# Hybrid attention and convolution block: some depthwise taps summed by adding transfers, attention cut into steps, plain pointwise products

## The chip, the core and the metric

One core of a Trainium2 chip runs the whole block once. The metric is device time in microseconds (us), from launch to end, as the median of several runs. Shapes are written partitions x elements. TensorE (PE) does matrix products, VectorE (DVE) and ScalarE (ACT) do elementwise work, GpSimd (POOL) does very little here, and SyncE (SP) issues the loads. PEld in the profile is TensorE's weight load, which runs beside its matmuls.

## What is computed

One layer over 256 tokens of width 4096, all in float32. Attention has 16 heads of 128; the convolution module has 2048 channels and 31 causal taps.

```python
xn   = rms_norm(h, norm_in_g)
proj = xn @ w_in                                  # 4096 -> 7 x 2048: q k v z_a a_c g_c z_c
y_a  = chunked_attention(q, k, v, rel_table)      # chunks of 64, all earlier chunks in the band
y_a  = rms_norm(y_a, attn_out_g) * silu(z_a)
u    = a_c * sigmoid(g_c)
u    = sum over k of w_dw[k] * u shifted by 30-k tokens, + b_dw      # depthwise, 31 taps
u    = silu(layer_norm(u))
y_c  = rms_norm(u @ w_pw + b_pw, conv_out_g) * silu(z_c)
h    = h + concat(y_a, y_c) @ w_out
h    = h + sigmoid(rms_norm(h) @ w_ple_gate + b) * (p @ w_ple)
out  = rms_norm(h, final_g)
```

## The kernel before

**Products.** Each float32 operand is split into a high part, which fits TensorE's fast float32 format, and the low rest; a product is three matmuls (high x high, low x high, high x low). `mixed_product` makes two column blocks of 512 at a time for all 256 tokens, over 16 *units* of 256 rows of the weight (8 units for the pointwise product). For a unit it loads two 512 KB tiles `wt` (128x1024), ACT casts each to `wh` (`parts_of`, L204) and DVE subtracts to get `wl` (L205). A plain unit has 24 matmuls of 512 columns. A unit marked `*` (a "seven") uses a Strassen-like scheme with 7 sub-products in place of 8, so 21 matmuls, and in exchange DVE makes sums of weights (`ua`, `ub`, L427 to L432) that are cast and subtracted too (`uh`, `ul`), and combinations of the left operand (`comb`). Buffers: five `wt`, three each of `wh` and `wl`, two each of `uh` and `ul`.

**Order of the work.** First come ten groups of `w_in` columns: `glu_conv(0)` and `(1)` (the convolution's input), `keys(0)`, `values(0)`, `attention(0)`, `glu_conv(2)` and `(3)`, `keys(1)`, `attention(1)`, `keys(2)`, then q and v (`attention(2)` after it), then k and v (`attention(3)` after it). Then the pointwise product with `w_pw` in two halves (`point`), four `gated` groups, four groups with `w_out` and four with `w_ple_gate`.

**Deferred work.** Small steps wait in the queue `later`; `fill(n)` pops n of them after each unit, n coming from a table such as `early_fills`. Each `glu_conv(c)` puts its 4 x 31 taps there (`conv_tap`, L681: one DVE instruction multiplies a shifted row block by a tap's weight and adds it to `cv`). `layer_norm_swish` puts the normalisation there: sums, `mean`, `center`, `square`, `variance`, `spread`, `swish` (ACT's Silu on 128x256, L785) and `split` (L795, L796), which makes the left operand `uS` of the pointwise product.

**Attention** handles 4 heads (`attention(g)`), head after head: scores on TensorE (L841, L842), scale, bias and maximum on DVE (L848, L852), Exp on ACT (L853), three transposes (L860), a copy by DVE (L862), the product with v (L865 to L867), a scaling by ACT (L869).

A scheduler fixes each engine's order when the program is built; it moves instructions past each other as dependences allow, except where `pin` keeps the program's order or `tc.issue_after(i)` puts the instructions of a block, on i's engine, behind i. At run time each engine runs its list strictly in order. Transfers issued by SP go in order too; each waits for its tile to be free. A tile is free when its last reader is done; `act` has eight buffers shared by `xin`, `cv`, `qT`, `y_c`.

Of the kernel before, what the change touches and what calls it, by code (L numbers as in the profile page):

```python
# [10 lines left out]
F32 = mybir.dt.float32  # L11
F32R = mybir.dt.float32r
AF = mybir.ActivationFunctionType
ALU = mybir.AluOpType
# [11 lines left out]
def hybrid_block(  # L26
# [152 lines left out]

    later = deque()  # L180

    def fill(n):
        for _ in range(min(n, len(later))):
            later.popleft()()

# [13 lines left out]
    def parts_of(wt, kc, tiles=None):  # L199
        if tiles is None:  # L200
            tiles = part_tiles()
        wh, wl = tiles
        made = (
            nc.scalar.copy(wh[:, :kc, :], wt[:, :kc, :]),  # L204
            nc.vector.tensor_tensor(  # L205
                wl[:, :kc, :], wt[:, :kc, :], wh[:, :kc, :].bitcast(F32), ALU.subtract
            ),
        )
        return (wh, wl), made

# [112 lines left out]

    early_fills = (4, 6, 7, 1, 5, 1, 5, 1, 5, 1, 2, 4, 6, 6, 6, 4)
    final = units("1 0* 3 2* 5 4* 6* 7 8* 9 10* 12* 11 13 14 15")
    late = units("1 3 5 7 9 11 13 15 0* 2 4* 6 8* 10* 12 14")

    def mixed_product(
# [67 lines left out]
        for n, (pair, seven) in enumerate(order):  # L396
# [9 lines left out]
            if n >= len(order) - n_left:  # L406
                for k in range(2):
                    tiles = left[2 * (n - len(order) + n_left) + k]
                    held.append((2 * pair + k, parts_of(wts[k], 2, tiles and tiles())[0]))
                fill(fills[n % len(fills)])  # L410
                continue
            if not seven:
                for k in range(2):
                    add_plain(n, k, *parts_of(wts[k], 2)[0])
                fill(fills[n % len(fills)])
                continue
# [39 lines left out]
            if n == last_seven:  # L456
                on_helpers(helper)
            fill(fills[n % len(fills)])
        after.close()
# [213 lines left out]
    conv = []  # L673

    def conv_tap(cv, uT, i, b, k):
        if k == PAD:
# [3 lines left out]
        else:  # L680
# [3 lines left out]
            )  # L684

    def glu_conv(c):
        if c == 0:
# [3 lines left out]
        else:  # L691
            sg, gate = scaled_pair(
                w_in0, o_a + c * NB, o_g - o_a, early, r_x, early_fills,
                
# [27 lines left out]
    def layer_norm_swish():  # L722
# [13 lines left out]
        def mean(s):  # L736

            m = tmp_psum()
            nc.tensor.matmul(m[:, :T], mean_w, fold(s), start=True, stop=True)
            stat("mu", m[:, :T])  # L740
# [20 lines left out]
        def variance(s):  # L761

            s = fold(s)
            m = tmp_psum()
# [6 lines left out]
            rsqrt(st["r"], m[:, :NH], 1)  # L771

        def spread(s):

            m = tmp_psum()
            for h in range(NH):
                d = s[:, 0, h * P : (h + 1) * P]
                nc.vector.tensor_scalar(d, ident, st["r"][:, h : h + 1], None, ALU.mult)
                nc.tensor.matmul(m[:, h * P : (h + 1) * P], mean_w, d, start=True, stop=True)
# [20 lines left out]
        later.extend(partial(total, c) for c in range(n))  # L800
        later.append(lambda: mean(st["s"]))
# [4 lines left out]
        later.append(lambda: variance(st["q"]))  # L806
        later.extend(rest)
        later.append(lambda: spread(st["s"]))
        later.extend(rest)
# [26 lines left out]
    def attention(g):  # L836
        qT, kT, v, bias = qs[g], ks.pop(g), vs.pop(g), biases.pop(g)
        y = qT.rearrange("q g (h d) -> q h g d", h=NH)
        for hd in range(GH):
# [4 lines left out]
            nm = spool.tile([P, NH], F32, tag="nm", name="nm")  # L844
            den = spool.tile([P, NH], F32, tag="den", name="den")
            for h, (lo, hi) in enumerate(((0, P), (P, P + T))):
# [8 lines left out]
                    accum_out=den[:, h : h + 1],  # L855
                )
            nc.vector.reciprocal(den, den)
            pt = tmp_psum()
            for j in range(3):
                nc.tensor.transpose(pt[:, j * P : (j + 1) * P], s[:, j * P : (j + 1) * P], ident)  # L860
            pT = spool.tile([P, 3 * P], F32, tag="pT", name="pT")
            nc.vector.tensor_copy(pT, pt[:, : 3 * P])  # L862
            o = tmp_psum()
            vc = slice(hd * HD, (hd + 1) * HD)
# [7 lines left out]
        for h in range(NH):  # L872
            square_sum(ssq_a[:, h, g : g + 1], y[:, h])
        y_a.append(y)
# [6 lines left out]
    def load_bias(g):  # L881
# [9 lines left out]
        )  # L891
        nc.gpsimd.memset(bias[: P // 2, :, : P // 2], NEG)

# [19 lines left out]
    def late_pool():  # L913
# [15 lines left out]
    load_bias(1)  # L929
    keys(1, early_fills)  # L930
    attention(1)
    keys(2, early_fills)
    layer_norm_swish()
    load_bias(2)
# [3 lines left out]
    k, vs[3] = blocks(  # L938
        (o_k + 3 * NB, o_v + 3 * NB), valued, (5, 5, 4, 5, 4, 2, 3, 2, 3, 2, 3, 4, 4, 4, 4, 4),
        then=late_pool,  # L940
    )
    keyed(3, k)
    attention(3)
    r_a = rstd_of(ssq_a, AW, "r_a")


# [10 lines left out]

    point = units("1 3 4 5 0* 6 2* 7"), units("0 1 2 3 4 5 6 7")
    uC = {}
    for c in range(2):  # L960
        uC[2 * c] = act.tile([P, 2, 2, T], F32R, tag="act", name="comb_u"), 0
        scratch = spool.tile([P, 2, NB], F32, tag="stage", name="comb")
        combine_again(*uC[2 * c], uS[c], 0, (scratch[:, 0], scratch[:, 1]))()
    first_scratch.close()
    spool = upool = pool("lpool", 2, side=1)
    y_c = []
    ssq_c = cpool.tile([P, NH, CW // NB], F32, name="ssq_c")
    for c0, order in zip(range(0, CW // NB, 2), point):
        row = broadcast_row(b_pw, c0 * NB, 2 * NB, tag="stage")
        rows = [row[:, j * NB : (j + 1) * NB] for j in range(2)]  # L970
        ys, z = [], []

        def y_tiles():
            ys.extend(act.tile([P, NH, NB], F32, tag="act", name="y_c") for _ in range(2))

        def on_helpers(helper):
            y_tiles()
            z.extend([ys[j][:, h, :] for j in range(2)] for h in range(NH))
            tt(z[0][0], helper["P1"], rows[0], ALU.add)
            helper_sums(helper, z)  # L980
            for h, j in QUARTERS[1:]:
                tt(z[h][j], z[h][j], rows[j], ALU.subtract if j else ALU.add)

        acc = mixed_product(w_pw[0], c0 * NB, uS, uC, order, on_helpers)
        if not z:
            y_tiles()
        for h, j in QUARTERS:
            y = ys[j][:, h, :]
            if z:
                tt(y, acc[h][j], y, ALU.subtract if j else ALU.add)  # L990
            else:
                tt(y, acc[h][j], rows[j], ALU.add)
            square_sum(ssq_c[:, h, c0 + j : c0 + j + 1], y)
        y_c.extend(ys)
    nc.scalar.activation(idle_out, ssq_c[:, 0, 1:2], AF.Silu)
    r_c = rstd_of(ssq_c, CW, "r_c")
# [304 lines left out]
```

## Time and profile before

| What | Value |
|---|---|
| Median of 3 runs | 2039.21 us (2038.81 to 2040.08) |
| The profiled execution | 2041.64 us, its span 2039.9 us |
| PE, PEld | 99%, 81% busy |
| DVE, ACT, POOL | 95%, 58%, 0% busy |
| Loads of weights and x | 406 MB read, 201 GB/s over the span; 16 transfer engines 63% busy |
| `w_in` groups after the first, about 80 to 880 us | DVE 773 us and ACT 428 us busy of 800 |
| Pointwise product, about 880 to 1000 us | DVE 103 us and ACT 74 us busy of 120 |

A row of a group gives line, engine, operation, tiles (out<-in), count, busy time and mean nanoseconds of one, then the engine's idle time before them and what ended it. A busy TensorE is not TensorE at its best: a 512-column matmul is recorded with some 390 ns but the next one starts long before it ends, so what counts is the distance between starts. `<-` in waits and timelines names what the waiting engine was released by.

### The profile page before, as it was taken

To read this page: it belongs to the slowest core of one execution; us is meant where nothing else is said; L and a number is where in the kernel's file an instruction comes from. 1 tells how busy PE (TensorE), PEld (TensorE's weight loads), DVE (VectorE), ACT (ScalarE), POOL (GpSimd) and SP (SyncE) were. 2 spreads that over 40 slices of the span, in tenths; PEclk is the share of its full clock that TensorE was granted. 3 is DMA by queue.
4 is the path that set the end of the run, shared out by engine and by line. 5 is a ranking of instruction groups with operands and counts; after the bars stand their busy time and mean duration, and the time that the engine had idled before them with its cause. 6 is when DMAs were issued, how large, how long until landed. Compare 5 with 4: busy or idle time off the path is not lost.

```text
span 2039.9 us, 26023 instructions
## 1 busy us (share of the span) xinstructions
PE 2018.6 (99%) x9088; PEld 1657.7 (81%) x9088; DVE 1929.4 (95%) x2760; ACT 1190.0 (58%) x1537; POOL 8.5 (0%) x19
## 2 busy tenths in 40 slices
PE   9999999999999999999999999999999999999997
PEld 7888888888888888877888888888888888888876
DVE  7999999989999999988899999999999999999998
ACT  7655545655555545576556556676565666655555
POOL 0000000000000000000000000000000000000000
PEclk9999999999999999999999999999999999999999
DMA  8666666566665666655666666676666656666765
GB/s 290 191 197 205 201 193 201 170 197 195 205 200 163 196 197 185 191 165 195 185 221 199 196 217 200 218 237 205 208 208 202 211 188 209 196 220 206 235 208 179
DMA packets 157758, 412.30 MB, mean 202 GB/s; under 512 B 12974, under 2 KB 16190, under 8 KB 157626
## 3 DMA queue, kind: packets, MB, share of 16 engines
q1 hardware_dynamic: 156976, 409.80, 63.2%
q8 instruction: 71, 1.16, 0.2%
q10 hardware_dynamic: 650, 0.84, 0.1%
q14 instruction: 61, 0.50, 0.1%
HBM read 406.39 MB, written 4.19 MB: 201 GB/s over the span
## 4 chain that ended last, share of the span: by engine, by line
PE 52%; DVE 2%; issue 1%; DMA 1%; ACT 0%; POOLq 0%; POOL 0%; ACTq 0%; DVEq 0%
PE acc L371 38%; PE acc_P L371 12%; PE acc L218 1%; DVE wl L205 1%; PE tmp_ps L170 1%; DMA wt<-in_w_in_dram 0%; DVE ul L205 0%; PE acc L359 0%; DMA wt<-in_w_out_dram 0%; ACT wh L204 0%; DVE ub L431 0%; DVE hc L1100 0%; DVE ua L428 0%; PE tmp_ps L860 0%; PE tmp_ps L842 0%
## 5 line engine op out<-in xcount | busy, mean ns | idle before, releaser
L371 PE MATMUL acc<-wh,big_t 128*128 128x512 f32 x4224 | 1308.3, 392 | 5.0 <-ACT wh L204 2.6
L204 ACT CAST wh<-wt 128x1024 fp32r<-128x1024 f32 (+1 forms) x737 | 711.8, 976 | 539.4 <-PE acc L371 401.5
L371 PEld LDWEIGHTS acc<-wh,big_t 128*128 128x128 f32 x4224 | 791.0, 188 | 169.8 <-ACT wh L204 4.5
L205 DVE TENSOR_TENSOR wl<-wt,wh 128x1024 fp32r<-128x1024 f32 (+1 forms) x737 | 819.9, 1124 | 36.2 <-ACT wh L204 32.3
L371 PE MATMUL acc<-wl,big_t 128*128 128x512 f32 x2112 | 814.7, 391 | 0.0
L371 PEld LDWEIGHTS acc<-wl,big_t 128*128 128x128 f32 x2112 | 396.5, 188 | 84.2 <-DVE wl L205 1.8
L204 ACT CAST uh<-ub 128x1024 fp32r<-128x1024 f32 x128 | 134.6, 1052 | 127.7 <-DVE ub L432 103.7
L681 DVE SCALAR_TENSOR_TENSOR cv<-uT,dw,cv 128x249 f32<-128x249 f32 (+22 forms) x480 | 207.6, 460 | 0.6
L204 ACT CAST uh<-ua 128x1024 fp32r<-128x1024 f32 x128 | 134.8, 1053 | 85.4 <-DVE ua L428 80.1
L205 DVE TENSOR_TENSOR ul<-ub,uh 128x1024 fp32r<-128x1024 f32 x128 | 156.0, 1219 | 8.4 <-ACT uh L204 7.8
L371 PE MATMUL acc_P<-uh,big_t 128*128 128x512 f32 x528 | 161.8, 392 | 0.0
L205 DVE TENSOR_TENSOR ul<-ua,uh 128x1024 fp32r<-128x1024 f32 x128 | 155.8, 1218 | 0.2 <-ACT uh L204 0.2
L371 PEld LDWEIGHTS acc_P<-uh,big_t 128*128 128x128 f32 x528 | 98.0, 188 | 23.0 <-ACT uh L204 3.4
L427 DVE TENSOR_TENSOR ua<-wt 128x512 f32<-128x512 f32 x128 | 87.7, 685 | 23.1 <-DMA wt<-in_w_in_dram 16.6
L371 PE MATMUL acc_P<-ul,big_t 128*128 128x512 f32 x264 | 101.6, 393 | 0.2
L428 DVE TENSOR_TENSOR ua<-wt 128x512 f32<-128x512 f32 x128 | 87.4, 683 | 5.7 <-DMA wt<-in_w_out_dram 3.1
L432 DVE TENSOR_TENSOR ub<-ub,wt 128x512 f32<-128x512 f32 x128 | 87.6, 684 | 0.8
L431 DVE TENSOR_TENSOR ub<-ua,wt 128x512 f32<-128x512 f32 x128 | 87.4, 683 | 0.3
L371 PE MATMUL acc<-uh,big_t 128*128 128x512 f32 x256 | 79.2, 390 | 0.0
L371 PE MATMUL acc_P<-wh,big_t 128*128 128x512 f32 x256 | 79.1, 389 | 0.0
L371 PE MATMUL acc_P<-uh,comb_t 128*128 128x512 f32 x228 | 70.2, 391 | 0.1
L371 PEld LDWEIGHTS acc_P<-ul,big_t 128*128 128x128 f32 x264 | 49.4, 188 | 13.6 <-DVE ul L205 3.3
(230 smaller groups left out, 1343.7 us busy)
## 6 DMA issues: line engine op xcount, KB each, us to landing
wt<-in_w_in_dram SPq DMA_DIRECT2D x447, 512.0 KB, 4.1
wt<-in_w_out_dram SPq DMA_DIRECT2D x128, 512.0 KB, 4.2
wt<-in_w_ple_gate_dram SPq DMA_DIRECT2D x128, 512.0 KB, 4.1
wt<-in_w_pw_dram SPq DMA_DIRECT2D x32, 512.0 KB, 4.8
hc<-in_x_dram SPq DMA_DIRECT2D x8, 512.0 KB, 6.0
wt<-in_w_ple_dram SPq DMA_DIRECT2D x8, 512.0 KB, 4.4
xin<-in_x_dram SPq DMA_DIRECT2D x7, 512.0 KB, 8.3
out_dram<-hc SPq DMA_DIRECT2D x12, 256.0 KB, 2.5
```

The costliest lines, as they stand in the source:

```text
L170: nc.tensor.transpose(pt[:, i * T + h * P : i * T + (h + 1) * P], src[:, h, b] if len(src.shape) == 4 else src[:, h, b * P : (b + 1) * P], ...
L204: nc.scalar.copy(wh[:, :kc, :], wt[:, :kc, :]),
L205: nc.vector.tensor_tensor(wl[:, :kc, :], wt[:, :kc, :], wh[:, :kc, :].bitcast(F32), ALU.subtract),
L218: nc.tensor.matmul(acc, a, b[:, k, :], start=kb == 0 and kind == 0, stop=kb == kblocks - 1 and kind == 2,)
L371: nc.tensor.matmul(banks[name], a, b, start=name not in begun, stop=final and ends[name] == n and kind == 2 and not (left and name in "P2 ...
L427: plus(ua[:, 0], w0[:, 0], w0[:, 1])
L428: plus(ua[:, 1], w0[:, 1], w1[:, 1])
L431: plus(ub[:, 0], ua[:, 0], w1[:, 1])
L432: plus(ub[:, 1], ub[:, 0], w1[:, 0])
L681: nc.vector.scalar_tensor_tensor(cv[:, i, PAD - k :], uT[:, i, : T + k - PAD], dw[:, b, k : k + 1], cv[:, i, PAD - k :], ALU.mult, ALU.add,)
```

## The change

1. **Taps as adding transfers.** Of each channel block's 31 taps, the shortest `ADDED[c]` (15, 15, 14 and 10 for c = 0 to 3) leave DVE. For such a tap ACT multiplies four shifted blocks by the tap's weights into one of two buffers `tap` (both from `act`), and POOL issues a transfer that adds the 512 KB buffer to `cv`. `add_one` issues one after two of every three units. A tap's buffer is reused two taps later, so ACT waits for that transfer's end; each transfer to a `cv` waits for the one before it.
2. **Deferred work tied.** What `fill` pops is put behind the latest cast `wh` on ACT's list.
3. **Attention in steps.** `attention(g)` queues five steps (`heads`), two heads at a time; `deal` pops one after each unit of the next group. The mask's `memset` of the bias moves into `attention` and is pinned on POOL.
4. **Plain pointwise groups.** The first half had two sevens; both halves are plain now, and the combinations `uC` are gone.
5. **Layer norm.** Its folds and the scaling of `ident` become steps of their own, with empty steps between; the fill tables are changed. `r_a` is made after the pointwise product.

```diff
+    def behind_casts():
+        return tc.issue_after(last_cast[0].ins) if last_cast else nullcontext()
+
     def fill(n):
-        for _ in range(min(n, len(later))):
-            later.popleft()()
+        with behind_casts():
+            for _ in range(min(n, len(later))):
+                later.popleft()()
+
+    def deal(n):
+        fill(n)
+        if heads:
+            with behind_casts():
+                heads.popleft()()
+
+    def add_one(n):
+        if adds and n % 3 < 2:
+            adds.popleft()()
...
-    early_fills = (4, 6, 7, 1, 5, 1, 5, 1, 5, 1, 2, 4, 6, 6, 6, 4)
+    early_fills = (4, 5, 5, 1, 4, 1, 4, 1, 4, 1, 2, 3, 4, 4, 4, 3)
+    more_fills = (6, 7, 7, 2, 6, 2, 6, 2, 6, 2, 4, 6, 8, 8, 8, 6)
...
-                fill(fills[n % len(fills)])
+                deal(fills[n % len(fills)])
+                add_one(n)
...
+    ADDED = (15, 15, 14, 10)
+    def conv_added(cv, uT, c):
+        held = []
+        def tap(k):
+            if k < 2:
+                held.append(act.tile([P, 4, T], F32, tag="act", name="tap"))
+                nc.gpsimd.memset(held[k][:, :, :PAD], 0.0)
+            t = held[k % 2]
+            for i in range(4):
+                b = 4 * c + i
+                pin(
+                    nc.scalar.activation(
+                        t[:, i, PAD - k :], uT[:, i, : T + k - PAD], AF.Identity,
+                        scale=dw[:, b, k : k + 1],
+                    )
+                )
+            nc.gpsimd.dma_start(cv, t, accum_op=ALU.add)
+        return [partial(tap, k) for k in range(ADDED[c])]
...
-            for k in reversed(range(TAPS)):
+            for k in reversed(range(ADDED[c], TAPS)):
                 later.append(partial(conv_tap, cv, uT, i, 4 * c + i, k))
+        later.append(lambda: adds.extend(conv_added(cv, uT, c)))
...
+        two = [(0, 1), (2, 3)]
+        heads.append(turn(*((scores, hd) for hd in two[0])))
+        heads.append(turn(*((turned, hd) for hd in two[0]), *((scores, hd) for hd in two[1])))
+        heads.append(turn(*((weighed, hd) for hd in two[0]), *((turned, hd) for hd in two[1])))
+        heads.append(turn(*((weighed, hd) for hd in two[1])))
+        heads.append(squares)
...
-    point = units("1 3 4 5 0* 6 2* 7"), units("0 1 2 3 4 5 6 7")
+    point = units("0 1 2 3 4 5 6 7")
```

Where this moves instructions, in three places. ACT's list from the layer norm's last statistic `rs` on; `cv<-cv,prm` is the swish, `z` the end of a product group, L795 the split. Before, at the end of the last `w_in` group:

```order
L734 ACTIVATE rs<-tmp_ps 128x256
L204 CAST wh<-wt 128x1024
L785 ACT_TABLE_LOAD
L785 ACTIVATE cv<-cv,prm 128x256 x7
L491 ACTIVATE z<-z,r_x 128x512 x3
L785 ACTIVATE cv<-cv,prm 128x256 x8
L204 CAST wh<-wt 128x1024
```

Now, where the group before that one ends and that group begins:

```order
L781 ACTIVATE rs<-tmp_ps 128x256
L836 ACT_TABLE_LOAD
L836 ACTIVATE cv<-cv,prm 128x256 x2
L222 CAST wh<-wt 128x1024
L836 ACTIVATE cv<-cv,prm 128x256 x4
L222 CAST wh<-wt 128x1024 x2
L836 ACTIVATE cv<-cv,prm 128x256 x4
L222 CAST wh<-wt 128x1024 x2
L836 ACTIVATE cv<-cv,prm 128x256
L222 CAST wh<-wt 128x1024 x2
L836 ACTIVATE cv<-cv,prm 128x256
```

Fifteen swishes stood between two casts; now at most four do. After the rows shown the last swishes alternate with the Exp of `attention(2)`, so that five table loads (Silu and Exp in turn) stand in this stretch; in the whole program there are 12, and 8 before.

TensorE's list in `attention(0)`, before (`s` the scores after Exp, `pT` their transposes):

```order
L371 MATMUL acc_3301<-wl,big_t 128x512
L860 MATMUL tmp_ps<-ident,s 128x128
L371 MATMUL acc_3303<-wh,big_t 128x512 x2
L860 MATMUL tmp_ps<-ident,s 128x128 x2
L371 MATMUL acc_3303<-wl,big_t 128x512
L371 MATMUL acc_3302<-wh,big_t 128x512 x2
L371 MATMUL acc_3302<-wl,big_t 128x512
L865 MATMUL tmp_ps<-z,pT 128x128
```

and now:

```order
L391 MATMUL acc_3244<-wl,big_t 128x512
L924 MATMUL tmp_ps<-ident,s 128x128 x6
L901 MATMUL tmp_ps<-kT,qT 128x128
L902 MATMUL tmp_ps<-kT,qT 128x256
L901 MATMUL tmp_ps<-kT,qT 128x128
L902 MATMUL tmp_ps<-kT,qT 128x256
L391 MATMUL acc_3241<-wh,big_t 128x512 x2
```

Before, 4 large matmuls stand between the last transposes of a head and the product that reads them; now 24 stand between the steps of a pair of heads.

ACT's list where `values(0)` ends and `glu_conv(2)` begins, with the new products `tap`:

```order
L510 ACTIVATE z<-acc_P_2691,r_x 128x512
L490 COPY z<-acc_P_2691 128x512
L222 CAST wh<-wt 128x1024 x2
L513 ACTIVATE z<-z,r_x 128x512
L222 CAST wh<-wt 128x1024
L513 ACTIVATE z<-z,r_x 128x512 x2
L722 ACTIVATE tap<-uT,dw 128x227 x4
L722 ACTIVATE tap<-uT,dw 128x228 x4
L222 CAST wh<-wt 128x1024 x2
L722 ACTIVATE tap<-uT,dw 128x229 x4
L222 CAST wh<-wt 128x1024 x4
```

Here three taps come within two casts: the third reuses the first one's buffer.

More of the change, by code (lines that the diff above doesn't have):

```diff
@@ L771, in variance, with diagonals @@
             rsqrt(st["r"], m[:, :NH], 1)
+        def diagonals(s):
+            for h in range(NH):
+                nc.vector.tensor_scalar(
+                    s[:, h * P : (h + 1) * P], ident, st["r"][:, h : h + 1], None, ALU.mult
+                )
         def spread(s):
@@ L837, in attention, with scores @@
         qT, kT, v, bias = qs[g], ks.pop(g), vs.pop(g), biases.pop(g)
+        pin(nc.gpsimd.memset(bias[: P // 2, :, : P // 2], NEG))
         y = qT.rearrange("q g (h d) -> q h g d", h=NH)
-        for hd in range(GH):
+        held = {}
+        def scores(hd):
             sp = tmp_psum()
@@ L871, in attention, with squares, turn @@
                 )
-        for h in range(NH):
-            square_sum(ssq_a[:, h, g : g + 1], y[:, h])
+        def squares():
+            for h in range(NH):
+                square_sum(ssq_a[:, h, g : g + 1], y[:, h])
+        def turn(*steps):
+            return lambda: [step(hd) for step, hd in steps]
+        two = [(0, 1), (2, 3)]
[4 more added lines that the diff above has]
+        heads.append(squares)
         y_a.append(y)
@@ L929, in hybrid_block @@
     load_bias(1)
-    keys(1, early_fills)
+    keys(1, more_fills)
     attention(1)
     keys(2, early_fills)
+    while adds:
+        adds.popleft()()
     layer_norm_swish()
@@ L956, in hybrid_block @@
     fill(len(later))
-    point = units("1 3 4 5 0* 6 2* 7"), units("0 1 2 3 4 5 6 7")
[L959 to L965, printed above, removed]
+    point = units("0 1 2 3 4 5 6 7")
     y_c = []
     ssq_c = cpool.tile([P, NH, CW // NB], F32, name="ssq_c")
-    for c0, order in zip(range(0, CW // NB, 2), point):
+    for c0 in range(0, CW // NB, 2):
         row = broadcast_row(b_pw, c0 * NB, 2 * NB, tag="stage")
[L970 to L986, printed above, removed]
+        acc = mixed_product(w_pw[0], c0 * NB, uS, None, point, None)
+        ys = [act.tile([P, NH, NB], F32, tag="act", name="y_c") for _ in range(2)]
         for h, j in QUARTERS:
             y = ys[j][:, h, :]
[L989 to L992, printed above, removed]
+            tt(y, acc[h][j], row[:, j * NB : (j + 1) * NB], ALU.add)
             square_sum(ssq_c[:, h, c0 + j : c0 + j + 1], y)
         y_c.extend(ys)
+        if c0 == 0:
+            assert not heads
+            first_scratch.close()
+            spool = upool = pool("lpool", 2, side=1)
+    r_a = rstd_of(ssq_a, AW, "r_a")
     nc.scalar.activation(idle_out, ssq_c[:, 0, 1:2], AF.Silu)
```

47 lines of the change are left out of this document (30 added, 17 removed).

## The prediction

> **What bounds the kernel now.** I read the shares first, then windows by stage, then what TensorE waits for in each, then the timeline at the longest wait.
>
> ```profile
> PE 2018.6 (99%) x9088; PEld 1657.7 (81%) x9088; DVE 1929.4 (95%) x2760; ACT 1190.0 (58%) x1537; POOL 8.5 (0%) x19
> core 0: us, PE busy (x) PEld busy (x) DVE busy (x) ACT busy (x) POOL busy (x), PEclk, DMA share, GB/s
> 80.00:880.00 800.00, 797.89 (x3615) 656.80 (x3614) 772.88 (x1217) 428.07 (x528) 2.31 (x5) 1.00 0.63 193
> 880.00:1000.00 120.00, 115.92 (x521) 92.97 (x520) 102.75 (x174) 74.46 (x126) 1.06 (x1) 0.99 0.55 181
> 1008.00 6.12 PE acc L371 x27
> ```
>
> TensorE is the bound everywhere. In an undisturbed stretch (the last row, from the chain) 27 large matmuls start in 6.12 us, 0.2267 us each; only matmuls taken away, or waits, can change the end. From 80 to 880 us VectorE is nearly a second bound: 772.88 of 800 us, 97%. What TensorE loses there shows best at its weight loads, first for 80 to 880, then for 880 to 1000 us (columns: total us, times, longest):
>
> ```profile
> PEld acc_P L371 <- DVE ul L205: 2.8, 6, 1.3
> PEld tmp_ps L860 <- ACT s L853: 2.6, 7, 0.4
> PEld tmp_ps L826 <- DVE z L495: 2.3, 4, 0.9
> PEld tmp_ps L865 <- DVE pT L862: 1.1, 7, 0.2
> PEld acc_P L371 <- ACT uh L204: 0.6, 2, 0.3
> ...
> PEld acc L371 <- DVE z L495: 0.4, 2, 0.2
> PEld acc L371 <- DVE wl L205: 0.3, 1, 0.3
> ...
> PEld acc L371 <- ACT wh L204: 3.1, 1, 3.1
> PEld tmp_ps L860 <- ACT s L853: 1.4, 5, 0.4
> PEld acc L371 <- DVE y_c L992: 1.1, 1, 1.1
> PEld acc L371 <- DVE y_c L990: 0.7, 1, 0.7
> ...
> PEld acc_P L371 <- DVE ul L205: 0.7, 2, 0.5
> PEld tmp_ps L865 <- DVE pT L862: 0.2, 1, 0.2
> ```
>
> All the change can win lies here: some 17 us in the rows shown. The longest wait, on ScalarE, and what follows it:
>
> ```profile
> 875.86 3.56 ACT L785 ACTIVATE cv<-cv,prm 128x256 f32<-128x256 f32 x7
> 879.33 1.94 ACT L491 ACTIVATE z<-z,r_x 128x512 f32<-128x512 f32 x3
> 881.17 4.03 ACT L785 ACTIVATE cv<-cv,prm 128x256 f32<-128x256 f32 x8
> 885.11 1.03 ACT L204 CAST wh<-wt 128x1024 fp32r<-128x1024 f32 x1
> 886.18 1.68 PE L371 MATMUL acc<-wh,big_t 128*128 128x512 f32 x6 [2.63 <-ACT wh L204]
> 886.18 15.54 PE acc L371 x60
> 888.00:890.00 2.00, 2.00 (x6) 1.54 (x5) 1.87 (x4) 2.00 (x5) 0.00 (x0) 0.50 0.58 203
> ```
>
> ScalarE is busy with fifteen swishes and three scalings from 875.86 to 885.20, and the next weight tile's cast comes after them. TensorE has nothing to multiply, and for a while after that the granted clock is 0.50: 60 matmuls take 15.54 us where 60 x 0.2267 = 13.6, so 1.9 us more.
>
> **The change, part by part.** The order of both programs gives the counts.
>
> *Swish (deferred work tied).* At most four swishes now stand between two casts, so this wait, 3.1 us, and the slow clock, 1.9 us, should go: 5.0 us. The bunch could re-form where the swishes now run, beside attention's Exp and five table loads; so the ends are 0 and -5.0. The longest run without a cast there is a table load and four Exps:
>
> ```profile
> L853 ACT ACTIVATE s<-s,nm 128x256 f32<-128x256 f32 x16 | 7.9, 494 | 0.0
> L853 ACT ACT_TABLE_LOAD x3 | 3.8, 1283 | 0.1
> ```
>
> That is at most 1.28 + 4 x 0.49 = 3.3 us. A cast tile feeds 12 matmuls, 2.7 us, and three buffers make 8.2: the old bunch, 9.3 us, was longer than the cover, the new ones are not. I take -4.5.
>
> *Plain pointwise.* Two sevens become plain: 2 x (24 - 21) = 6 matmuls, 6 x 0.2267 = +1.4 us, on TensorE's path, covered by nothing. The wait for `ul` (0.7) goes. The wait for `y_c` at the end of the half (L990, 0.7) becomes one like the other half's (L992, 1.1), since DVE now does the same four additions there. Together +1.4 - 0.7 + 0.4 = +1.1; ends +0.4 and +1.4.
>
> *Attention in steps.* The rows for `s` and `pT` sum to 2.6 + 1.1 + 1.4 + 0.2 = 5.3 us: transposes that follow an Exp by a few matmuls. With 24 matmuls between steps, 24 x 0.2267 = 5.4 us, two heads' chain of scale, maximum, Exp and copy fits if DVE and ACT come to it at once, and not if they are in a backlog of casts. Ends 0 and -5.3; I take two thirds, -3.5.
>
> *Taps off DVE.* 54 steps of 4, so 216 DVE instructions:
>
> ```profile
> L681 DVE SCALAR_TENSOR_TENSOR cv<-uT,dw,cv 128x226 f32<-128x226 f32 x16 | 7.1, 446 | 0.0
> L681 DVE SCALAR_TENSOR_TENSOR cv<-uT,dw,cv 128x240 f32<-128x240 f32 x16 | 7.4, 460 | 0.0
> L156 ACT ACTIVATE big_t<-tmp_ps,prm 128x256 fp32r<-128x256 f32 x64 | 27.7, 470 | 4.1 <-DVE big_t L157 2.5 <-PE tmp_ps L170 1.6
> L204 ACT CAST wh<-wt 128x1024 fp32r<-128x1024 f32 x609 | 632.7, 1051 | 454.6 <-PE acc L371 347.2 <-DVE cv L681 20.0 <-ACT uh L204 17.5
> ```
>
> The removed ones are the first two rows' shapes and those between: 216 x 0.453 = 98 us of DVE, which falls from 97% to (773 - 98)/800 = 84%. That is not time of the kernel: TensorE was only made to wait for DVE by `ul`, `z` and `wl`, 2.8 + 2.3 + 0.4 + 0.3 = 5.8 us in 80 to 880. The `z` waits come at a group's end, where DVE must wait for the last matmul in any case. Ends 0 and -5.8; I take half, -2.9.
>
> *Products on ACT, additions by transfers.* ACT gets 216 x 0.470 = 102 us (the scaling of a 128x256 block, third row, is nearest), and goes from 54% to 66% of the 800 us. It was idle 347.2 us before casts because their buffers were still being read by TensorE (fourth row), so on average this is free. What can cost is place: a tap's four products take 1.9 us, and in a seven ACT has 0.62 + 3 x 1.05 = 3.8 us of casts in 21 x 0.2267 = 4.8 us. Of a group's four sevens (units 4, 6, 8, 10) three are followed by an add, in some 4.5 groups: 13 places where `uh` may come late. The trace shows no add, but a late `uh` cost 0.6 us in 2 times, 0.3 each. All 13 would be +3.9; if instead the full excess 3.8 + 1.9 - 4.8 = 0.9 hit each, +12. Buffers ahead of TensorE cover part: ends 0 and +12; I take half of 3.9, +1.9.
>
> *The rest.* The layer norm's folds are the same work in more steps, hidden under the same products; `r_a` is used only in deferred steps of the `gated` groups; the masks' `memset` are part of POOL's 2.31 us from 80 to 880. But POOL now has a queue: the mask of `attention(0)` stands behind 20 adds, and DVE's score step waits for it, with all of DVE's list behind that. And `qT` takes `act` buffers that taps held. Both cost nothing as long as adds land at their pace.
>
> Sum: -4.5 + 1.1 - 3.5 - 2.9 + 1.9 = -7.9 us, against the profiled execution's 2041.64 us, so 2033.7. That execution lies 2.4 us above the median of 2039.21; from the median it is **2031.3 us**.
>
> **Rivals.**
>
> *Adds land too late (slower).* A group of 12 plain units and 4 sevens takes (288 + 84) x 0.2267 = 84.3 us and has 11 adds, one in 7.7 us. Adds follow one another, each after the last has landed, and ACT waits for the one two back with all casts behind it. ACT's own slack per add is 34% of 7.7, 2.6 us; from 10.3 us an add, TensorE waits. The nearest rows, by median us from issue to landing:
>
> ```profile
> wt<-in_w_in_dram SPq DMA_DIRECT2D x447, 512.0 KB, 4.1
> hc<-in_x_dram SPq DMA_DIRECT2D x8, 512.0 KB, 6.0
> xin<-in_x_dram SPq DMA_DIRECT2D x7, 512.0 KB, 8.3
> ```
>
> An add reads two blocks of 512 KB where `wt` reads one: between 4.1 and, twice, 8.2 us, and twice the middle row is 12.0. I take 7, below 7.7. Each 0.1 us over 10.3 costs 54 x 0.1 = 5.4 us: at 10.5, 10.8 us, and 2031.3 + 10.8 = 2042; at 12.0 it would be 92 us more, 2123. Against it: the transfer engines are 63% busy, so there is room.
>
> [...]
>
> *DVE's relief and the steps change nothing (no change).* If TensorE's small waits only move to the next late cast, -2.9 and -3.5 fall away: -4.5 + 1.1 + 1.9 = -1.5, so 2037.7. For it: the waits are 0.1 to 0.4 us each, about the length of a missed slot. Against: with 13% of DVE freed, `wl` runs ahead.
>
> *All of it works (faster still).* With the favourable ends and no cost on ACT: -5.0 + 0.4 - 5.3 - 5.8 = -15.7, so 2023.5. Against it: `z` waits are there whatever DVE's load.
>
> **Numbers.** Less than 0.2% (4.1 us) is about what runs of this kernel cannot tell from no change. The forecast (2025 to 2035) 0.54, all works 0.12, no change 0.19 (up to 2043.3), adds too late 0.10; 0.05 for smaller losses on ACT, `uh` late by the full 0.9 us in every seven (+12 in place of +1.9) with attention unimproved: -4.5 + 1.1 - 2.9 + 12 = +5.7, 2045. So faster 0.68 (with 0.02 of the no-change case at the border), same 0.17, slower 0.15. The range reaches from 2024, near the favourable end, to 2043, where the no-change case ends; it leaves out most of the two slower cases and little below. The forecast's own range is 2025 to 2035.
>
> **What would show it.** DVE near 84% from 80 to 880 us; in the pointwise stage no wait near 3 us and the granted clock 1.00; waits for `s` and `pT` under 2 us in all; adds landing in 5 to 8 us; no long wait of ACT for `tap`'s transfers. The prediction is wrong if adds take over 10 us, if ACT's new load leaves TensorE waiting for `wh` or `uh` by several us, or if a wait on POOL's mask appears on DVE.

## The result: 31 us slower, and where they went

The changed kernel took 2070.89 us (median of 4 runs, 2067.26 to 2080.92), the kernel before 2039.64 beside it: a ratio of 1.0153, 95% interval 1.0136 to 1.0170. The profiled execution after took 2073.29 us, its span 2071.5.

Windows of the kernel after, in the columns of the prediction's table; then two stretches of the kernel before and the same two after. Adds run from 202 to 754 us only.

```profile
80.00:880.00 800.00, 772.25 (x3453) 628.05 (x3451) 673.24 (x974) 496.77 (x736) 52.04 (x65) 1.00 0.77 219
880.00:1000.00 120.00, 119.95 (x554) 99.45 (x553) 86.77 (x127) 68.80 (x109) 0.69 (x1) 1.00 0.61 196
```

```profile
200.00:480.00 280.00, 279.80 (x1267) 231.37 (x1266) 270.27 (x428) 147.55 (x178) 0.00 (x0) 1.00 0.63 191
520.00:760.00 240.00, 239.05 (x1091) 197.00 (x1090) 237.31 (x386) 122.20 (x151) 0.61 (x2) 1.00 0.63 194
```

```profile
200.00:480.00 280.00, 266.58 (x1184) 216.55 (x1183) 212.16 (x286) 180.78 (x288) 27.20 (x35) 0.99 0.85 235
520.00:760.00 240.00, 225.70 (x1006) 180.96 (x1005) 201.35 (x302) 149.48 (x241) 21.57 (x27) 0.99 0.84 229
```

VectorE fell to 673 of 800 us, 84%, as worked out. The stage from 880 to 1000 us, which had lost 4 us, loses nothing. (All work comes some 30 us later now, so that the pointwise product lies at about 910 to 1030 us; there too TensorE is busy 119.93 of 120 us.) But TensorE is busy 26.6 us less where adds run (13.2 and 13.4), and there the transfer engines went from 63% to 85%. Idle time isn't all of the loss: the two stretches hold 2022 large matmuls in place of the 2190 before, and 168 x 0.2267 is 38 us, an estimate. Part of the difference is the clock, as in the place below, where the granted clock is 0.50 from 308 to 310 us, behind a stop. The 880 to 1000 us window gives some of the 38 us back. What waited from 80 to 880 us (total us, times, longest):

```profile
DVE wl L223 <- ACT wh L222: 61.1, 47, 4.0
ACT tap L722 <- DMA cv<-tap: 37.6, 16, 4.5
PEld acc L391 <- DVE wl L223: 27.2, 24, 3.3
DVE ua L448 <- DMA wt<-in_w_in_dram: 24.8, 14, 4.3
PE acc L391 <- DVE wl L223: 17.9, 17, 2.9
DVE ua L449 <- DMA wt<-in_w_in_dram: 15.5, 12, 3.0
```

Before, the row of `ua` waiting for a load was this, and TensorE's waits for `wl` were 0.3 us:

```profile
DVE ua L427 <- DMA wt<-in_w_in_dram: 4.5, 7, 1.0
```

One such place, in the timeline of VectorE and then TensorE after:

```profile
300.64 0.69 DVE L223 TENSOR_TENSOR wl<-wt,wh 128x512 fp32r<-128x512 f32 x1
305.61 0.69 DVE L448 TENSOR_TENSOR ua<-wt 128x512 f32<-128x512 f32 x1 [4.28 <-DMA wt<-in_w_in_dram]
306.22 1.22 DVE L223 TENSOR_TENSOR wl<-wt,wh 128x1024 fp32r<-128x1024 f32 x1
...
307.49 0.80 PE L391 MATMUL acc<-wl,big_t 128*128 128x512 f32 x1 [2.86 <-DVE wl L223]
```

ScalarE made three casts `wh` from 301.44 to 304.37 us. As far as the casts go, the `wl` that TensorE needs could have come earlier, but VectorE's list has the `ua` of the next seven ahead of it, and `ua` waits 4.28 us for its load. The loads and the adds between 200 and 480 us, by queue (packets, MB, share of 16 engines) and by median us from issue to landing, before and then after:

```profile
q1 hardware_dynamic: 23542, 53.27, 62.4%
wt<-in_w_in_dram SPq DMA_DIRECT2D x102, 512.0 KB, 4.1
```

```profile
q1 hardware_dynamic: 21759, 49.84, 53.5%
q0 software_dynamic: 4320, 15.73, 30.8%
wt<-in_w_in_dram SPq DMA_DIRECT2D x96, 512.0 KB, 5.0
cv<-tap POOLq DMA_DIRECT2D x30, 512.0 KB, 6.1
```

An add takes 0.308 x 280 / 30 = 2.87 us of all 16 engines, a load of the same size 0.535 x 280 / 96 = 1.56. Loads land 0.9 us later. From issue to landing the 54 adds took:

```profile
DMA to landing us min/median/max: 4.5/6.2/9.2
```

### The profile page after: what moved, and what is told of

It is laid out like the page before. It is cut to its first block, busy times and chain, and to the rows that moved or that the text cites. A ratio compares the mean times of both kernels' runs of the same rounds, so it can differ in the third digit from the quotient of the medians.

```text
span 2071.5 us, 26157 instructions
## 1 busy us (share of the span) xinstructions
PE 2028.1 (98%) x9094; PEld 1661.2 (80%) x9094; DVE 1841.2 (89%) x2512; ACT 1268.1 (61%) x1750; POOL 58.1 (3%) x81
## 4 chain that ended last, share of the span: by engine, by line
PE 82%; DVE 8%; DMA 6%; issue 3%; ACT 2%; POOLq 0%; DVEq 0%; POOL 0%; ACTq 0%; SPq 0%
PE acc L391 64%; PE acc_P L391 13%; DMA wt<-in_w_in_dram 4%; DVE wl L223 3%; DMA cv<-tap 2%; DVE cv L705 1%; PE tmp_ps L170 1%; DVE ul L223 1%; PE acc L237 1%; ACT wh L222 1%; ACT tap L722 0%; DVE ub L452 0%; PE tmp_ps L902 0%; DVE ua L449 0%; DVE ub L453 0%
## 5 line engine op out<-in xcount | busy, mean ns | idle before, releaser
L705 DVE SCALAR_TENSOR_TENSOR cv<-uT,dw,cv 128x252 f32<-128x252 f32 (+16 forms) x264 | 117.6, 474 | 0.6
L722 ACT ACTIVATE tap<-uT,dw 128x226 f32<-128x226 f32 (+14 forms) x216 | 88.0, 479 | 37.6 <-DMA cv<-tap 37.6
```

Source lines behind the costliest of these rows:

```text
L705: nc.vector.scalar_tensor_tensor(cv[:, i, PAD - k :], uT[:, i, : T + k - PAD], dw[:, b, k : k + 1], cv[:, i, PAD - k :], ALU.mult, ALU.add,)
L722: nc.scalar.activation(t[:, i, PAD - k :], uT[:, i, : T + k - PAD], AF.Identity, scale=dw[:, b, k : k + 1],)
```

## Experiments

Theory A: the adds' traffic makes weight loads late, and VectorE's list stands at `ua` with a `wl` behind that TensorE needs. Rival B: ScalarE waits for the add two back with its casts behind. Rival C: the products on ScalarE. Rival D: another part of the change. Ratios are to the kernel before, run beside them (medians of 2040.56 to 2041.05 us); they differ by up to 0.07% from the quotient of the two medians.

**Products without transfers.**

```diff
-            nc.gpsimd.dma_start(cv, t, accum_op=ALU.add)
```

> The changed kernel with its 216 tap products on ScalarE kept and the 54 adding transfers (and with them ScalarE's wait for the add two back) left out, so that 54 taps are missing from the sum. Theory A (the transfers' traffic makes weight loads late, VectorE's list stands at a copy that needs the load, TensorE behind it): the loss goes, 2026 to 2036 us, loads land at the median of 4.1 us again between 200 and 480 us. Rival B (ScalarE waits for the add two back and the casts behind it are late): the wait goes with the transfers too, 2026 to 2036 us; this run doesn't part it from A. Rival C (ScalarE's products themselves, 88 us of them, are what makes the casts late): the loss stays, 2060 to 2072 us. Rival D (another part of the change, the tied deferred work or attention in steps): the loss stays, 2060 to 2072 us.

2040.61 us, ratio 0.9999 (0.9990 to 1.0008). C and D fall: without transfers the loss is gone, and loads land in 4.2 us from 200 to 480 us. But nothing is won either; the time lies 4.6 us above what A and B gave. The waits of 80 to 880 us in this run tell which of the rows above are loss:

```profile
DVE wl L223 <- ACT wh L222: 61.9, 49, 4.0
DVE ua L448 <- DMA wt<-in_w_in_dram: 17.5, 14, 2.5
PEld acc L391 <- DVE wl L223: 7.4, 14, 1.2
DVE ua L449 <- DMA wt<-in_w_in_dram: 4.7, 6, 1.8
```

VectorE has less to do and waits more; its wait for casts is as long as in the changed kernel, and `ua` waits 22.2 of the 40.3 us, without much of it coming through to TensorE. The transfers add 18 us to the waits of `ua`, and 20 us to TensorE's for `wl` (27.2 against 7.4).

**Transfers without products.**

```diff
-                nc.gpsimd.memset(held[k][:, :, :PAD], 0.0)
+                nc.gpsimd.memset(held[k], 0.0)
...
-            for i in range(4):
-                b = 4 * c + i
-                pin(nc.scalar.activation(t[:, i, PAD - k :], uT[:, i, : T + k - PAD], AF.Identity, scale=dw[:, b, k : k + 1]))
-            nc.gpsimd.dma_start(cv, t, accum_op=ALU.add)
...
+            pin(nc.scalar.activation(tick, uT[:, 0, :NH], AF.Identity, scale=dw[:, 4 * c, k : k + 1]))
...
+            pin(nc.gpsimd.tensor_tensor(junk2, tick, mhalf, ALU.add))
+            pin(nc.gpsimd.dma_start(cv, t, accum_op=ALU.add))
```

> The changed kernel with the 54 adding transfers kept at their places and ScalarE's 216 tap products and its wait for earlier adds left out: what is added is a tile of zeros, and one small ScalarE operation paces each transfer. 54 taps are missing from the sum. Theory A (the traffic delays the weight loads): the loss stays, 2055 to 2072 us, with VectorE's copies waiting for loads about as in the changed kernel (24 and 13 waits, 55 us together). Rival B (ScalarE's wait for the add two back): gone, 2026 to 2038 us. Rival C (the products on ScalarE): gone, 2026 to 2038 us. Rival D (another part): stays, 2060 to 2072 us, but with no more waits for loads than before.

2059.25 us, 1.0096 (1.0081 to 1.0111): A's case. Waits of `ua` for a load, 80 to 880 us, 46 us together where the changed kernel has 40 (the 55 us of the expectation are of the whole program):

```profile
DVE ua L448 <- DMA wt<-in_w_in_dram: 36.6, 14, 5.8
DVE ua L449 <- DMA wt<-in_w_in_dram: 9.5, 8, 3.1
```

**All taps back on VectorE, the rest of the change kept.**

```diff
-    ADDED = (15, 15, 14, 10)
+    ADDED = (0, 0, 0, 0)
...
-    early_fills = (4, 5, 5, 1, 4, 1, 4, 1, 4, 1, 2, 3, 4, 4, 4, 3)
-    more_fills = (6, 7, 7, 2, 6, 2, 6, 2, 6, 2, 4, 6, 8, 8, 8, 6)
+    early_fills = (4, 6, 7, 1, 5, 1, 5, 1, 5, 1, 2, 4, 6, 6, 6, 4)
+    more_fills = early_fills
```

> The changed kernel with no tap on ScalarE and none added by transfer: all 31 taps of each group are VectorE's again, at the rates of the lists of numbers before; the other parts of the change stay (attention in steps, deferred work tied to the last casts, plain pointwise groups, the normalization's sums split). Theories A, B and C: the loss of 200 to 760 us is gone, and what stays is the gain of the other parts, 2027 to 2036 us. Rival D (the loss belongs to one of the other parts): 2055 us or more.

The last two `w_in` groups have their lists of before too, 5 a unit and (5, 5, 4, 5, 4, 2, 3, 2, 3, 2, 3, 4, 4, 4, 4, 4). 2036.03 us, 0.9980 (0.9970 to 0.9989): 0.2% below the kernel before, and 1.7% below the changed one. It is called the run at 2036 below.

**Half of the adds.**

```diff
-        if adds and n % 3 < 2:
+        if adds and n % 3 < 1:
...
-    ADDED = (15, 15, 14, 10)
+    ADDED = (8, 8, 7, 5)
```

> The changed kernel with 28 taps of the four groups on ScalarE and by transfer in place of 54, one add after one unit of three in place of two of three, and VectorE's rates between the two lists. Theory A (traffic, so that a load is late when its neighbours in time are adds): with half as many adds in the same stretch, less than half of the loss, 2034 to 2052 us. Rival B (the wait for the add two back, each add now having twice the time): no loss, 2028 to 2036 us, with no wait of ScalarE for an add. Rival C (products): half of the loss, 2045 to 2055 us. Rival D: 2060 us or more.

2059.00 us, 1.0086 (1.0069 to 1.0102): slower than A, B or C had it, and just under D's 2060. The list of numbers `early_fills` was changed as well, to values between the two lists. A wait of its own came in, at 732 us: a copy into a `qT` whose buffer had been a `tap`, with TensorE's longest wait for a `wl`, 8.2 us, behind it.

```profile
DVE qT L888 <- DMA cv<-tap: 9.2, 1, 9.2
```

Less that, some 2050 by estimate: inside A's range, and C's too. The run can't say more.

**`ua` behind the copies of the group ahead (the reordered run).**

```diff
+        last_sub[:] = made[1:]                # the last wl made
...
+            subs = list(last_sub)
             w0h, w0l = parts_of(w0, 1)[0]
-            plus(ua[:, 0], w0[:, 0], w0[:, 1])
-            plus(ua[:, 1], w0[:, 1], w1[:, 1])
+            with behind_subs(subs):           # tc.issue_after(subs[0].ins)
+                plus(ua[:, 0], w0[:, 0], w0[:, 1])
+                plus(ua[:, 1], w0[:, 1], w1[:, 1])
```

> The changed kernel, with the two sums `ua` of a group of seven queued on VectorE behind the weight copy `wl` of the group ahead, where before they could stand ahead of it. Transfers and products stay. Theory A1 (a late load stops TensorE because `ua` waits for it at the head of VectorE's list while the copy behind it, whose load has long landed, is what TensorE needs): the wait of a plain group's copy goes and with it half of the 34 us by which the changed kernel stands above the run with all taps on VectorE, 2040 to 2058 us. Theory A2 (the loads that a group itself needs come too late, whatever the order): no better than 2063 to 2075 us.

2056.84 us, 1.0077 (1.0062 to 1.0092): 14 us back, with every product and transfer in place. In the first stretch all of it came back, at an even higher share of the transfer engines:

```profile
200.00:480.00 280.00, 279.61 (x1266) 231.63 (x1265) 230.14 (x315) 191.21 (x298) 27.18 (x35) 1.00 0.89 247
520.00:760.00 240.00, 230.60 (x1032) 186.35 (x1031) 202.54 (x297) 149.31 (x238) 21.57 (x27) 0.99 0.86 236
```

So there the late load costs by its place in VectorE's list. In the second stretch 9.4 us are still lost; one piece of it: at 540 us ScalarE's products wait 3.54 us for an add, with the activation `z` behind them that TensorE's transposes need.

```profile
540.04 1.61 ACT L728 ACTIVATE tap<-uT,dw 128x228 f32<-128x228 f32 x4 [3.54 <-DMA cv<-tap]
541.56 1.03 ACT L225 CAST wh<-wt 128x1024 fp32r<-128x1024 f32 x1
542.50 1.14 ACT L749 ACTIVATE z<-z 128x512 f32<-128x512 f32 x2
...
543.15 1.29 DVE L750 TENSOR_TENSOR z<-z 128x512 f32<-128x512 f32 x2 [2.88 <-ACT z L749]
```

**Transfers that copy, and transfers of half the bytes.** Both start from the run with transfers alone.

```diff
-            pin(nc.gpsimd.dma_start(cv, t, accum_op=ALU.add))
+            pin(nc.gpsimd.dma_start(cv, t))                                 # first run
+            pin(nc.gpsimd.dma_start(cv[:, :2], t[:, :2], accum_op=ALU.add)) # second run
```

> As the run with transfers alone (2059 us), but each of the 54 transfers copies its tile of zeros over the group instead of adding it, so that the four groups' sums are lost. Same bytes, same places. Theory A with the price in the addition (an adding transfer has to read what it adds to; in the changed kernel 30 of them took 30.8% of 280 us on 16 engines, 2.87 us each, where 96 loads of the same size took 53.5%, 1.56 us each): a copy takes about 1.5 us of the engines, loads are less late, 2038 to 2050 us. Theory A with the price in the bytes: 2054 to 2064 us.

> As the run with transfers alone (2059 us), but each of the 54 adds only two of the four blocks, 256 KB in place of 512. Theory A (the share of the transfer engines makes loads late): the loss of 23 us against the run with all taps on VectorE falls to less than half, 2037 to 2047 us. Rival E (it is the number of transfers, their issue on GpSimd or the order that VectorE and the transfers keep with each other on the same tile): stays, 2054 to 2064 us.

2045.14 us, 1.0020 (1.0011 to 1.0030), and 2044.88, 1.0020 (1.0011 to 1.0030). Queue q0 from 200 to 480 us, copies and then half adds:

```profile
q0 software_dynamic: 4320, 15.73, 14.8%
```

```profile
q0 software_dynamic: 4320, 7.87, 17.2%
```

A copy takes 1.38 us of the engines, about half of an add's 2.87. The kernel's time goes with that share: 15% and 17% give 2045, 32.4% (adds alone) 2059, none 2038 (below). The number of transfers is 54 in all three, so it can't make the 14 us between them; whether it has a part in the other 7 us isn't shown.

**Pointwise product as before.** With all taps on VectorE.

```diff
-    point = units("0 1 2 3 4 5 6 7")
+    point = units("1 3 4 5 0* 6 2* 7"), units("0 1 2 3 4 5 6 7")
...
+    while heads:
+        heads.popleft()()
```

The combinations `uC`, the helper sums and the change of scratch pool stand where they stood before.

> The changed kernel with all taps on VectorE again, and with the pointwise product as before the change too: two groups of seven in its first half, so 6 matmuls of 0.227 us fewer, the combined activations built and the scratch pool changed ahead of it, and the last head group's attention steps issued together ahead of it. Against 2036 us: by the prediction's terms the undone plain groups give back 1.1 us, and the steps that can no longer be spread cost up to 3.5 us, so 2035 to 2040 us. If the gain of the rest of the change lies mostly in the tied deferred work: 2034 to 2037 us.

2041.75 us, 1.0003 (0.9993 to 1.0012): worse than forecast. The plain groups, with all that goes with them, and the last attention's steps between them, are worth 0.23% together, the whole gain of the run at 2036. TensorE's waits of 880 to 1000 us show where, first undone, then at 2036 (where no row of `s` or `pT` is left):

```profile
PEld acc L391 <- ACT wh L222: 2.9, 1, 2.9
PEld tmp_ps L924 <- ACT s L913: 2.9, 7, 1.2
PEld acc L391 <- DVE wl L223: 1.7, 3, 1.0
PEld tmp_ps L933 <- DVE pT L926: 1.1, 3, 0.6
```

```profile
PEld acc L391 <- ACT wh L222: 2.9, 1, 2.9
PEld acc L391 <- DVE y_c L1046: 0.9, 2, 0.7
```

The wait for the swishes, 2.9 us, stands in both, with the tie in both.

**Neither products nor transfers.**

```diff
         def tap(k):
+            pass
-            if k < 2:
...
-            nc.gpsimd.dma_start(cv, t, accum_op=ALU.add)
```

> The changed kernel with both ScalarE's products and the transfers left out, so that 54 taps are missing from the sum; VectorE has 216 operations fewer, and its lists of numbers are those of the changed kernel. The run that keeps the products came to 2040.6 us, 4.6 above the run with all taps on VectorE. If the products on ScalarE cost that (88 us of them, casts behind them): 2030 to 2036 us here. If the lists of numbers cost it (six to eight taps a unit in the fourth group's stretch, set close between the weight copies, around 500 to 620 us): 2038 to 2042 us.

2038.44 us, 0.9983 (0.9974 to 0.9993). So the relief of VectorE, with the changed lists, wins nothing over the run at 2036, and the products cost 0.16% more, some 3 us, which these intervals barely part from none. From 880 to 1000 us this run loses 0.4 us where the run at 2036 loses 2.7, since the swishes come early. It gives that back where the changed lists set the remaining taps close: from 480 to 520 us VectorE is busy all the time and TensorE loses 1.9 us (0.4 at 2036), from 560 to 640 us 2.0 (none at 2036).

```profile
480.00:520.00 40.00, 38.07 (x162) 29.57 (x161) 40.00 (x61) 22.06 (x25) 0.00 (x0) 1.00 0.55 169
```

**Products that wait for no transfer.**

```diff
+            none, t = held          # transfers add a tile of zeros; products go into t
-            nc.gpsimd.dma_start(cv, t, accum_op=ALU.add)
+            pin(nc.gpsimd.dma_start(cv, none, accum_op=ALU.add))     # paced by a tick, as above
```

> As the run with transfers alone (2059.2 us; a tile of zeros is added each time), and with ScalarE's 216 products too, written into a tile that no transfer reads, so that no product waits for an earlier add. 54 taps are missing from the sum. The changed kernel stands 11.6 us above the run with transfers alone. Rival B (ScalarE's wait for the add two back is what makes that up): 2058 to 2064 us here. If the products themselves, beside the transfers, make it up: 2067 to 2074 us.

2057.63 us, 1.0078 (1.0062 to 1.0095). This is just under B's range, and no slower than the transfers alone: the products cost nothing that shows beside them. What the changed kernel has above this run, 13 us, is left to B, ScalarE's wait for the add two back (37.6 us in the changed kernel), which has no row here any more.

**Additions by GpSimd.**

```diff
-            nc.gpsimd.dma_start(cv, t, accum_op=ALU.add)
+            nc.gpsimd.tensor_tensor(cv, cv, t, ALU.add)
```

> The changed kernel with each of the 54 additions done by GpSimd (one operation over 128 partitions x 1024) in place of a transfer; nothing is left out. Theory A: with no transfers the weight loads are as before, and what stays is the run without transfers: 2036 to 2044 us, if an addition on GpSimd takes less than the 8 to 10 us between two adds and leaves VectorE's copies at 1.13 us. If VectorE and GpSimd hinder each other: copies of more than 1.3 us while an addition runs, 2046 to 2070 us.

2110.55 us, 1.0334 (1.0316 to 1.0353): far beyond the expected range. VectorE's instruction on 128x241 took as long as GpSimd's addition beside it. The two rows of this run that start together, and the same shape in the run without transfers:

```profile
287.94 2.62 DVE L705 SCALAR_TENSOR_TENSOR cv<-uT,dw,cv 128x241 f32<-128x241 f32 x1
...
287.94 2.35 POOL L727 TENSOR_TENSOR cv<-cv,tap 128x1024 f32<-128x1024 f32 x1 [2.34 <-ACT tap L722]
```

```profile
515.03 0.46 DVE L705 SCALAR_TENSOR_TENSOR cv<-uT,dw,cv 128x241 f32<-128x241 f32 x1
```

So VectorE was slower beside these additions: 2.62 us against 0.46 for that instruction; and from 200 to 760 us a `wl` of 128x1024 took 1.44 us on average, against 1.22 without transfers. What it depends on isn't shown.

**`ua` behind the copies, all taps on VectorE.** The same edit as in the reordered run.

> The run with all taps on VectorE (2036.0 us) with `ua` queued behind the copies of the group ahead, as in the run at 2056.8 us. There the waits of `ua` for a load were 55 us before the reordering; with no transfers they are 6 us, and TensorE loses only some 6 us in 80 to 880 us. So no more than 2 us to gain or lose: 2034 to 2038 us.

2043.31 us, 1.0009 (0.9999 to 1.0018): a miss; the reordering costs 7 us where no load is late. From 880 us to the end, where sevens follow each other with no adds about, TensorE now waits for `uh` and `ul`, whose `ua` comes later (4.0 and 1.2 us in the run at 2036):

```profile
PEld acc_P L395 <- ACT uh L225: 7.1, 25, 0.9
PEld acc_P L395 <- DVE ul L226: 6.8, 24, 0.5
```

**Statistic ready earlier; then the same without the tie.** Both with all taps on VectorE. The first changes the lists of the last two `w_in` groups of that run (two arguments), the second the tie as well:

```diff
-    (5,)        (5, 5, 4, 5, 4, 2, 3, 2, 3, 2, 3, 4, 4, 4, 4, 4)
+    (6,)        (5, 5, 4, 5, 3, 0, 0, 0, 0, 0, 0, 4, 4, 4, 4, 4)
...
-        return tc.issue_after(last_cast[0].ins) if last_cast else nullcontext()   # second run only
+        return nullcontext()
```

> The run with all taps on VectorE (2036.0 us), with two lists of numbers changed: six deferred steps a unit in place of five in the group before the last, and fewer in the last one, so that the layer norm's statistic `rs` is ready before the last group and at most four swishes stand between two casts. The run at 2036.0 us still had the bunch of 14 swishes and a wait of TensorE of 2.9 us at 881 us, with the tie in place. If the lists of numbers decide this wait: it goes, with the slow clock behind it, 2031 to 2034 us. If VectorE, 97% busy, can't take the steps earlier, so that `rs` comes late all the same: 2035 to 2038 us.

> As the run with the swishes' statistic ready early, with the tie left out: deferred steps and attention's steps may be moved ahead of the last cast. If the tie does what the prediction credited it with: 2 to 5 us slower than that run, with a wait of TensorE for a cast near 3 us. If the numbers alone do it: within 2 us of it.

2037.05 us, 0.9983 (0.9974 to 0.9992), and 2036.15, 0.9979 (0.9970 to 0.9988). `rs` is made at 828.8 and 828.3 us (870.6 at 2036), and the wait for the swishes is gone in both, so the numbers decide it; the tie, with these numbers, does nothing that can be measured. No time is won, so neither forecast of the first run held whole: what 880 to 1000 us gains, 760 to 880 us gives back. At 2036, TensorE was busy 119.4 us there and 117.3 in the next window. In the earlier one it now waits at its weight loads for `wl` (2.5 us), `uh` (1.9) and the layer norm's sum (0.9). The run with the tie:

```profile
760.00:880.00 120.00, 116.80 (x539) 95.53 (x538) 109.21 (x168) 74.85 (x109) 0.95 (x2) 1.00 0.60 182
880.00:1000.00 120.00, 119.71 (x554) 99.40 (x553) 87.62 (x143) 70.16 (x116) 1.38 (x2) 1.00 0.58 190
```

**Both mechanisms away, products and transfers kept.** The run whose products wait for no transfer, with `ua` behind the copies too.

> The run with transfers of zeros and products that wait for no transfer (2057.6 us), with `ua` queued behind the copies of the group ahead as well. 54 taps are missing from the sum. If traffic acting through `ua` and ScalarE's wait are the whole loss: what stays is the run with neither products nor transfers (2038.4 us), the products (2 us) and what the reordering cost without transfers (7 us), so 2043 to 2050 us; in 200 to 640 us TensorE loses no more than 12 us. If something else of the transfers is left: 2053 us or more.

2048.53 us, 1.0040 (1.0026 to 1.0053), inside the forecast. From 200 to 480 us nothing is lost at 89% of the transfer engines:

```profile
200.00:480.00 280.00, 279.93 (x1267) 231.60 (x1266) 236.42 (x329) 196.09 (x329) 44.88 (x63) 1.00 0.89 248
```

The 10 us above the run with neither products nor transfers are about what the products (2 to 3) and the reordering (7) cost by themselves. They don't all lie there, though. From 520 to 760 us this run loses 5.2 us where that one loses 2.0, and what makes the other 3 us stays open:

```profile
520.00:760.00 240.00, 234.75 (x1063) 191.37 (x1063) 209.07 (x309) 157.43 (x266) 36.19 (x50) 1.00 0.87 242
```

## Why the prediction was wrong, point by point

By the runs' ratios the change adds up so, each step uncertain by 0.1 to 0.25%: all but the taps -0.20%; VectorE's relief with the changed lists +0.03; products +0.16; transfers (from the run with products alone to the one whose products wait for no transfer) +0.79; ScalarE's wait for them (from there to the changed kernel) +0.75. That is +1.53%, 31 us; the prediction said -0.4%. The last two shares hold for this order of steps only. Putting `ua` behind the copies takes 0.76% off the changed kernel, freeing the products takes 0.75, and both together 1.13: some 0.4%, 8 us, are common to both waits.

- **Products on ACT, additions by transfers (+1.9, ends 0 and +12): the step that failed.** The products came near the term, some 3 us. (TensorE's waits for `uh`, which the term priced, rose from 0.6 to 7.2 us in 80 to 880 us, but 5.1 us stand there with no products too. And the 347.2 us of ScalarE's idle time before casts are of the whole program; from 80 to 880 us they are 218.3, still more than the products' 102.) The adds had been priced only by their landing, taken as 7 us (6.2 measured, 9.2 at most), and by whether ScalarE has slack for it on average: "from 10.3 us an add, TensorE waits". It waited below that, 16 times and 37.6 us in all, because adds come after two units of three and not evenly: two in a row stand 24 x 0.2267 = 5.4 us apart where the unit is plain, less than a landing, and 27 of the 54 stood on GpSimd behind the add before them (171 us). A wait of up to 4.5 us then has all casts behind it. The larger omission is in the words "the transfer engines are 63% busy, so there is room": an add took 1.8 times a load's share of the engines, 85% were busy, and loads came 0.9 us later at the median. No term asked which engine stands at a load with other work queued behind.
- **The rival that adds land too late** had the right sign and named one of the two waits that the runs found, ScalarE's. Its price hung on a landing of over 10 us, which never came, so its chance of 0.10 was given to the wrong condition.
- **Taps off DVE (-2.9):** 84% was right, the gain was not. With neither products nor transfers nothing came of it, as the rival of no change had it. In the 40 us shown VectorE was busy throughout and TensorE lost more than before; there it counts when each `wl` is made, and not how busy VectorE is on average.
- **Swish (-4.5):** the wait went in the changed kernel, but not for the reason given. With the tie and all taps on VectorE it stands; with other numbers it goes, tie or no tie. What decides is when the statistic `rs` is ready: 872 us before and 871 with all taps on VectorE, with the wait; 826 in the changed kernel and 828 to 829 with other numbers, without it. Where VectorE has to be early for that, the price came back in the stage ahead.
- **Plain pointwise (+1.1) and attention in steps (-3.5):** right together, and undersized in the pointwise stage alone: undoing both there costs 0.23%, 4.7 us, against a net -2.4 forecast for all stages. The waits for `s` and `pT` are gone there, as said. What the earlier attention groups give wasn't parted off by a run. At 2036 their waits for `s` and `pT` (2.6 and 1.1 us in 80 to 880 us) have no row any more either, but TensorE's busy time there rises by 0.3 us only, from 797.89 to 798.19.

## What to carry to other kernels

Price a new transfer by the time it takes of the transfer engines (here an adding one took 2.87 us, twice a copy's 1.38), and then look through each engine's list for an instruction that waits for a load with other engines' work queued behind it: a load that comes 1 us later can cost far more there (here loads landed 0.9 us later at the median, and `ua` waited up to 4.3 us). Relieving an engine that was 97% busy won nothing here, as the bound engine hardly waited for it, and the work that was left went to where the lists of numbers put it. An engine's longest waits need not be the loss: compare them with a run that has no loss. An in-order list has no right order by itself: the reordering that gave back 14 us under the adds cost 7 us without them.

## What the runs showed of the hardware

- A transfer that adds 512 KB within the on-chip memory took 2.87 us of all 16 transfer engines (3.02 in the run of transfers alone), one that adds 256 KB 1.6, one that copies 512 KB 1.38, a load of 512 KB from DRAM 1.56.
- GpSimd's addition over 128x1024 took 2.35 us in the row shown and 2.97 on average, and VectorE's tap on 128x241, 0.46 us in the run without transfers, took 2.62 when it started together with one.
- GpSimd's issue of an adding transfer took 0.86 to 1.04 us, and the add landed 4.5 to 9.2 us after it, 6.2 at the median; a copy of 512 KB landed after 5.5 us at the median, from 200 to 480 us.
- Three products of 128x256 from high and low parts, 768 columns, take 0.35 us from the first one's start to the start behind them (L359 of the kernel before, 2022.95 to 2023.30 us); 768 columns of scores in plain float32 take 1.12 us (L901 and L902 of the changed kernel, 378.19 to 379.31 us).
